# Gate logits as 2x2 block products of seven, their results summed in DRAM, in a one-core Trainium2 layer kernel

## The chip, the cores and the metric

The kernel runs on one core of a Trainium2 chip. It is one layer of a network in one launch, all in fp32, with every input and output in DRAM. The metric is the device time of the core in microseconds (us), lower is better. The engines are called as in the profile: PE is TensorE, DVE is VectorE, ACT is ScalarE, POOL is GpSimd, SP is SyncE, which issues most of the DMA transfers.

## The reference

The layer has 1024 tokens of 1024 channels. What matters here is its first sub-layer, two token mixers on one normalised input, each of them weighted by a gate per token and channel:

```python
h = rms_norm(x, norm_mix_pre)
proj = h @ w_in                 # q, k, v, u: 512 columns each; gate_logits: 2048
gate_attn, gate_ssm = jnp.split(jax.nn.sigmoid(gate_logits + b_gate), 2, axis=-1)
o_attn = stick_breaking_attention(q, k, v)      # 8 heads of 64
o_ssm = s5_branch(u, ...)       # 32 groups of 16 channels, 64 complex states; GELU, GLU
merged = gate_attn * (o_attn @ w_branch_attn) + gate_ssm * (o_ssm @ w_branch_ssm)
x = x + rms_norm(merged @ w_out, norm_mix_post)
```

Cross-attention into 256 memory tokens and a gated FFN with a causal convolution follow; the change leaves them as they are.

## The kernel before, in words

**Arithmetic.** A fp32 product is made of three matmuls on rounded operands: an operand is split into a high part, which ACT rounds, and a low part, which DVE makes as the difference; then come high x high, high x low and low x high (mm3, lines 141 to 143). One step of a projection is these three matmuls for 128 rows of the contraction, 128 output columns and 512 tokens. hT holds the normalised input, transposed, high and low. The norm's gain is in it, and the rate of a token (the reciprocal of its root mean square) is multiplied in later.

**A job** (class Job) is 128 columns of w_in: its weights are loaded (a tile ws), rounded (L255, ACT) and their low part is made (L259, DVE); 2 halves of 512 tokens by 8 steps of the contraction follow. There are 16 gate chunks, gate_job(0) to gate_job(15), 16 steps each. At the end of a half ACT copies the PSUM bank into a tile glog (L288), and SP stores it to g_d in DRAM. The merge, much later, loads g_d, multiplies the rates in and takes the sigmoid.

**The order of the work is written out by time.** at(t, go) puts a piece of work on a list with a planned time, and each engine's instructions are issued in the order of these times. The plan's times only set the order; on the chip an engine waits in that order for whatever its next instruction needs. Gate jobs are the filling between small matmuls that depend on other engines. Seven gate chunks fill the SSM (EARLY_SSM, 112 steps) and nine the attention (EARLY_ATT, 144 steps), in which the q and k projections fill too (128 steps).

**The stages**, by the profile's time: the v projection to 52 us; the projection of u, the SSM's input, to 92, beside which DVE prepares tables, operators and readouts of the SSM; the SSM to 218; the GLU to 241; the attention to 538; memory keys and values to 585; the merge to 673; then output projection, cross-attention and FFN.

**The SSM** goes in eight slots, one for four groups of channels (planned SLOT apart). In a slot: flip_u and flip_w (transposes); states (L732), eight matmuls; scan on DVE (L741 to L753), which reads their PSUM; outputs (L766, L767), planned 9.5 us after states, which read the scan's result rc. ACT puts the outputs through Gelu (L772). Every second slot, flip_y transposes eight blocks back (L783) and ACT copies them to U (L785). Between the slots' own work, for two slots at a time, DVE makes readout(n) (F, L678 to L680, three operations), operators(o) (W, L668 to L670, six operations) and tables(o) (cos and sin, L652 to L658, DVE and ACT). After the last flip_y, ACT and DVE split y into yh (L913) and yl (L916) for the GLU, whose matmuls are again lines 141 to 143.

**The attention** goes head by head. For each block of 256 queries: scores (L1004, L1005, PE), two sigmoids (L1016, L1017, ACT), a scan (L1022, DVE), a product (L1028, "rest", POOL), transposes (L1042, PE), the split of the weights into wth (L1049, ACT) and wtl (L1054, DVE), weigh (L1067, PE). Between these, in a fixed proportion, stand the fill steps.

Of the kernel before, what the change touches and what calls it, by code (L numbers as in the profile page):

```python
# [11 lines left out]
F32 = mybir.dt.float32  # L12
# [18 lines left out]
EARLY_SSM = (8, 9, 10, 11, 12, 13, 14)  # L31
EARLY_ATT = ((15, 0), (1, 2), (3, 4), (5, 6, 7))
# [13 lines left out]
def kernel(ctx: ExitStack, tc: tile.TileContext, a: dict, out: bass.AP, dbg=None):  # L46
# [35 lines left out]
    row_k = pr_.tile([P, 512], F32, name="row_k")  # L82
    rx_d = dpool.tile([KT, P], F32, name="rx_d")
# [199 lines left out]
    def gate_job(gi):  # L283
        def out(t, h, sl, acc):
            def put(t):
                pool, tag, bufs = logs[-1]
                gt = pool.tile([P, 512], F32, tag=tag, name="glog", bufs=bufs)
                C.copy(gt, acc)  # L288
                dma(g_d[gi][:, sl], gt)

            at(t, put)

        return Job(a["w_in_T"][8 + gi], out)

    def qk_job(pp, key):
# [28 lines left out]
        def start():  # L324

            qk[pp] = [[pqk.tile([P, S], F32R, tag=f"{n}{i}", name=f"{n}{i}") for i in range(2)] for n in ("q", "k", "kl")]
# [18 lines left out]
    px = wx.enter_context(tc.tile_pool(name="px", bufs=1, side="left"))  # L345
    rf, ra = ExitStack(), ExitStack()
    rf.enter_context(banks(f=(512, 2)))
    ra.enter_context(banks(keep="f", m=(512, 6)))
# [6 lines left out]
    logs.append((pa, "vt", 1))  # L355
# [7 lines left out]
    def x_load(t, kk=None):  # L363

        if t not in xt:
            xt[t] = p0.tile([P, KT, P], F32, tag="xt", name="xt", bufs=4)
# [7 lines left out]
    def w_load(n, c):  # L374
        raw[n, c] = px.tile([P, 1024], F32, tag="wr", name="wr", bufs=4)
        dma(raw[n, c], a["w_in_N"][n, c])
# [114 lines left out]
    def mem_load(i):  # L491
        raw["m", i] = px.tile([P, 1024], F32, tag="wr", name="wr", bufs=4)
# [11 lines left out]
    line(70.0, (lambda: mem_load(0), 0), (lambda: mem_load(1), 16.0), (lambda: mem_rate(0), 1.4), (lambda: mem_rate(1), 2.6),  # L504
# [132 lines left out]
    def open_t():  # L637
        r0.close()
        open_t.pool = rt.enter_context(tc.tile_pool(name="pt", bufs=1, side="right", reuse_waits="tile"))

    def tables(now, o):

        pool = open_t.pool
        x = pool.tile([P, 8, P], F32, tag="x", name="x")
        home, n_ = (open_b.pool, 1) if o == 2 else (pool, 2)
        cosT = home.tile([P, 8, P], F32, tag="cosT", name="cosT", bufs=n_)
        sinT = home.tile([P, 8, P], F32, tag="sinT", name="sinT", bufs=n_)
        tabs[o] = cosT, sinT
        G.memset(x[:, :, 0:1], 0.0)
# [1694 lines left out]
```

## Time and profile before

| | us |
|---|---|
| median of 3 runs (lowest, highest) | 1656.69 (1655.31, 1657.93) |
| span of the profiled execution | 1653.9 |
| PE busy | 1633.8 (99%) |
| DVE busy | 1163.6 (70%) |
| ACT busy | 880.1 (53%) |
| POOL busy | 202.2 (12%) |

The profile is of one further execution; its own time is its span, 1653.9 us from the first to the last instruction. A matmul's printed length includes its way through the array, so PE rows overlap: the distance between starts is what one costs. A window row gives, for a stretch of time, the busy time and the number of instructions of each engine, then PE's granted clock as a share of full speed (PEclk), the busy share of the DMA engines and what they moved. A row of the groups of instructions gives line, engine, operation, written and read tiles, shape and count, then busy us and the mean ns of one, then the idle time of the engine ahead of them and what ended it. In the chain, each row is one link: its start, its length and the work.

### The profile page before, as it was taken

To read this page: it belongs to the slowest core of one execution; us is meant where nothing else is said; L and a number is where in the kernel's file an instruction comes from. 1 tells how busy PE (TensorE), PEld (TensorE's weight loads), DVE (VectorE), ACT (ScalarE), POOL (GpSimd) and SP (SyncE) were. 2 spreads that over 40 slices of the span, in tenths; PEclk is the share of its full clock that TensorE was granted. 3 is DMA by queue.
4 is the path that set the end of the run, shared out by engine and by line. 5 is a ranking of instruction groups with operands and counts; after the bars stand their busy time and mean duration, and the time that the engine had idled before them with its cause. 6 is when DMAs were issued, how large, how long until landed. Compare 5 with 4: busy or idle time off the path is not lost.

```text
span 1653.9 us, 22415 instructions
## 1 busy us (share of the span) xinstructions
PE 1633.8 (99%) x8062; PEld 1379.8 (83%) x8062; DVE 1163.6 (70%) x1616; ACT 880.1 (53%) x1459; POOL 202.2 (12%) x296
## 2 busy tenths in 40 slices
PE   9999999999999999999999999999999999999998
PEld 7998887888888988888888888888888888888886
DVE  6778637776866687467655678888887788775473
ACT  5434346676766544344444556656565556654441
POOL 5000002333332000011000000111111111000010
PEclk9999999999999999999999999999999999999999
DMA  9412144232433954464423574677777676688672
GB/s 323 124 46 66 61 144 110 71 102 80 113 99 127 336 190 136 158 211 158 141 69 129 205 271 175 187 210 211 214 195 206 186 203 185 210 311 280 192 237 81
DMA packets 125439, 279.26 MB, mean 169 GB/s; under 512 B 23696, under 2 KB 28304, under 8 KB 125200
## 3 DMA queue, kind: packets, MB, share of 16 engines
q1 hardware_dynamic: 113664, 251.35, 46.1%
q0 software_dynamic: 9360, 18.09, 6.3%
q10 hardware_dynamic: 2304, 8.39, 1.3%
q8 instruction: 63, 1.03, 0.3%
q14 instruction: 48, 0.39, 0.1%
HBM read 203.98 MB, written 67.38 MB: 164 GB/s over the span
## 4 chain that ended last, share of the span: by engine, by line
PE 89%; DVE 6%; DMA 2%; ACT 2%; issue 1%; POOL 0%; SPq 0%; DVEq 0%; POOLq 0%; ACTq 0%
PE ps_p L1921 8%; PE ps_p L1919 8%; PE ps_p L1920 8%; PE ps_f L141 7%; PE ps_f L143 7%; PE ps_f L142 6%; PE ps_d L2190 4%; PE ps_d L2189 4%; PE ps_d L2191 4%; PE ps_m L141 3%; PE ps_m L143 3%; PE ps_m L142 3%; PE ps_o L1067 2%; PE ps_w L1042 2%; PE ps_z L141 1%; PE ps_z L142 1%
## 5 line engine op out<-in xcount | busy, mean ns | idle before, releaser
L141 PE MATMUL ps_f<-hT,wh 128*128 128x512 f32 x384 | 161.3, 420 | 0.0
L143 PE MATMUL ps_f<-hT,wl 128*128 128x512 f32 x384 | 150.8, 393 | 0.0
L142 PE MATMUL ps_f<-hT,wh 128*128 128x512 f32 x384 | 150.6, 392 | 0.0
L1920 PE MATMUL ps_p<-qS,bm 128*128 128x512 f32 (+2 forms) x368 | 140.4, 382 | 1.7 <-DVE qS L1744 1.7
L1919 PE MATMUL ps_p<-qS,bm 128*128 128x512 f32 (+2 forms) x368 | 140.5, 382 | 1.4 <-DVE uu L1937 0.9
L1921 PE MATMUL ps_p<-qS,bm 128*128 128x512 f32 (+2 forms) x368 | 140.5, 382 | 0.0
L147 DVE TENSOR_TENSOR dn<-raw,dn 128x1024 fp32r<-128x1024 f32 x77 | 93.4, 1223 | 63.0 <-ACT dn L146 59.2
L146 ACT CAST dn<-raw 128x1024 fp32r<-128x1024 f32 x77 | 80.5, 1054 | 87.2 <-PE ps_d L2191 36.4
L2189 PE MATMUL ps_d<-dn 128*128 128x512 f32 x308 | 119.8, 389 | 0.0
L2190 PE MATMUL ps_d<-dn 128*128 128x512 f32 x308 | 119.8, 389 | 0.0
L2191 PE MATMUL ps_d<-dn 128*128 128x512 f32 x308 | 119.8, 389 | 0.0
L1028 POOL TENSOR_TENSOR s<-s,s 128x127 f32<-128x127 f32 (+4 forms) x96 | 89.9, 937 | 223.8 <-DVE s L1022 178.6
L1921 PE MATMUL ps_p<-qA,bm 128*128 128x512 f32 (+2 forms) x272 | 105.1, 386 | 0.5 <-DVE bm L1850 0.5
L1919 PE MATMUL ps_p<-qA,bm 128*128 128x512 f32 (+2 forms) x272 | 105.3, 387 | 0.0
L1920 PE MATMUL ps_p<-qA,bm 128*128 128x512 f32 (+2 forms) x272 | 105.0, 386 | 0.0
L1932 ACT COPY uu<-ps_p 128x512 f32<-128x512 f32 (+2 forms) x90 | 51.5, 572 | 90.0 <-PE ps_p L1921 90.0
L1862 POOL DMA_DIRECT2D bm<-in_ffn_up_T x61 | 52.7, 864 | 356.6 <-ACT bm L1861 144.2
L143 PEld LDWEIGHTS ps_f<-hT,wl 128*128 128x128 f32 x384 | 72.1, 188 | 16.3
L1016 ACT ACTIVATE s<-ps_z,rates_x 128x128 f32<-128x128 f32 (+3 forms) x96 | 56.3, 587 | 54.0 <-PE ps_z L1005 47.8
L1919 PEld LDWEIGHTS ps_p<-qS,bm 128*128 128x128 f32 x368 | 69.2, 188 | 15.2 <-ACT uu L1932 2.2
L1920 PEld LDWEIGHTS ps_p<-qS,bm 128*128 128x128 f32 x368 | 69.2, 188 | 15.1 <-DVE qS L1744 2.0
L1921 PEld LDWEIGHTS ps_p<-qS,bm 128*128 128x128 f32 x368 | 69.3, 188 | 13.2
(544 smaller groups left out, 4462.2 us busy)
## 6 DMA issues: line engine op xcount, KB each, us to landing
raw<-sd SPq DMA_DIRECT2D x77, 256.0 KB, 3.5
bm<-in_ffn_up_T POOLq DMA_DIRECT2D x61, 256.0 KB, 5.4
ws<-in_w_in_T SPq DMA_DIRECT2D x24, 512.0 KB, 3.3
ws<-in_xa_wo_N SPq DMA_DIRECT2D x23, 512.0 KB, 4.3
wv<-in_ffn_up_T SPq DMA_DIRECT2D x22, 512.0 KB, 4.0
wg<-in_ffn_up_T SPq DMA_DIRECT2D x22, 512.0 KB, 3.8
dr<-in_ffn_down SPq DMA_DIRECT2D x22, 512.0 KB, 6.4
td<-st SPq DMA_DIRECT2D x44, 256.0 KB, 5.9
```

Source lines behind the costliest of these rows:

```text
L141: T.matmul(acc, sh, mh, start=first, stop=False)
L142: T.matmul(acc, sh, ml, start=False, stop=False)
L143: T.matmul(acc, sl, mh, start=False, stop=last)
L146: C.copy(dh, src)
L147: (lo or V).tensor_tensor(dl, src, f(dh), op=ALU.subtract)
L1028: G.tensor_tensor(s1[:, n0:e], s1[:, n0:e], s2[:, n0 + 1:e + 1], op=ALU.mult)
L1919: T.matmul(acc, bm[:, 0, ks], q[:, 0, k, cs], start=alone and k == 0, stop=False, skip_group_check=True)
L1920: T.matmul(acc, bm[:, 0, ks], q[:, 1, k, cs], start=False, stop=False, skip_group_check=True)
L1921: T.matmul(acc, bm[:, 1, ks], q[:, 0, k, cs], start=False, stop=k == 3, skip_group_check=True)
L2189: T.matmul(acc[i], v[:, 0, 0, sl], v[:, 0, 1], start=first, stop=False, skip_group_check=True)
L2190: T.matmul(acc[i], v[:, 0, 0, sl], v[:, 1, 1], start=False, stop=False, skip_group_check=True)
L2191: T.matmul(acc[i], v[:, 1, 0, sl], v[:, 0, 1], start=False, stop=last, skip_group_check=True)
```

## The change: gate chunks by pairs, seven products for eight

Two gate chunks (a pair: m = 0, 1), two halves of the tokens (th = 0, 1) and two halves of the contraction (4 steps each) are a 2x2 product of blocks. The new class Product does one of Strassen's seven products of such a pair: four steps of three matmuls (L428) on a sum of weight blocks and a sum of input blocks. 8 pairs x 7 products x 4 steps are 224 steps where there were 256.

- **Weight sums**: the second block is added by an accumulating load that POOL issues; for product 1 DVE makes the difference. Then ACT rounds (L401, L403) and DVE makes the low part (L407, L409), on 128x512.
- **Input sums** ("quads", for products 1, 2, 5, 6 and 7; 3 and 4 use hT): one at a time, from a new input x_Q, in one slot of a new pool that the x tiles of the first stage share. For 7 and 6 the second block is added by an accumulating load, and ACT and DVE scale and split. For 2, 5 and 1 ACT scales (4 operations), DVE adds (4), ACT rounds (4), DVE makes the low part (4).
- **Results**: a product goes to one or two of the four blocks of g_d. ACT copies it with its sign (L439, L441); the first contribution to a block is a plain store of SP, later ones are accumulating stores that POOL issues (52 of 54 of them in the attention). A copy whose two places have the same sign serves both. Odd chunks are kept negated, and the sigmoid's scale mends that. In the SSM products 4 and 7, or 3 and 6, of a pair share one PSUM accumulator and are copied once.
- **Places**: the SSM has 28 products (4, 7, 3, 6), 112 steps as before; the attention has 28 (first 2, with the q and k jobs between, then 5, then four of 3, then 1), 112 steps in place of 144.
- **To make room**: SLOT is 13.6 in place of 12.2, and outputs are planned 10.5 us after states in place of 9.5. readout 2 and 3 and operators 2 move from the u stage into SSM slots, tables 2 and 3 into slots 1 and 3. W has 2 buffers (3), F1 2 (4); r shares bp, x shares sinT, tq shares bt. PSUM m has 5 banks (6), a new g has 1. glog has 3 buffers in the SSM (1) and 2 in the attention as before. Some attention and memory tiles share buffers, and the merge's stage tiles are opened 25 us earlier.

```diff
-    def gate_job(gi):
...
+            for hh, d in enumerate(parts):
...
+    class Product:
...
+        def total(self, t):
+            if self.n == 1:
+                V.tensor_tensor(self.ws, self.ws, self.whole[:, 512:], op=ALU.subtract)
+            elif len(FACTOR[self.n]) == 2:
+                G.dma_start(self.ws, self.source(1), accum_op=ALU.add)
...
+            for j, (st, mv_) in enumerate(((wh, mh), (wh, ml), (wl, mh))):
+                T.matmul(self.acc, st, mv_, start=self.chain != "ends" and k == 0 and j == 0, stop=k == 3 and j == 2,
+                         skip_group_check=True)
...
+                gt = pool.tile([P, 512], F32, tag=tag, name="glog", bufs=bufs)
+                if sign < 0:
+                    C.mul(gt, self.acc, -1.0)
+                else:
+                    C.copy(gt, self.acc)
+                for th, m, adds in places:
+                    dst = g_d[2 * self.i + m][:, th * 512:(th + 1) * 512]
+                    if adds:
+                        at(t + 1.5, lambda _, dst=dst: G.dma_start(dst, gt, accum_op=ALU.add))
+                    else:
+                        dma(dst, gt)
...
-    SLOT = 12.2
+    SLOT = 13.6
...
-            plan(s0 + 9.5, 1.75, outputs, n)
+            plan(s0 + 10.5, 1.75, outputs, n)
...
-            if n == 0:
-                at(s0 + 8.5, lambda t: operators(t, 3))
-            if n == 1:
-                at(s0 + 8.5, lambda t: tables(t, 3))
+            if n in (0, 2):
+                at(s0 + 8.5, lambda t, n=n: operators(t, 2 + n // 2))
+            if n in (1, 3):
+                at(s0 + 8.5, lambda t, n=n: tables(t, 2 + n // 2))
...
+    quad(2, "w", clock + 9.0, (0.0, 13.0), 8.0)
...
+    fill_products(phase[3])
+    fill_products(phase[1])
```

On PE, at the end of the SSM, the order before was this (y is the last Gelu's output, hT and wh, wl a gate job's operands):

```order
L767 MATMUL ps_m<-F_1577,rc 128x128
L141 MATMUL ps_f<-hT_119,wh 128x512
L142 MATMUL ps_f<-hT_121,wh 128x512
L143 MATMUL ps_f<-hT_119,wl 128x512
L141 MATMUL ps_f<-hT_119,wh 128x512
L142 MATMUL ps_f<-hT_121,wh 128x512
L143 MATMUL ps_f<-hT_119,wl 128x512
L783 MATMUL ps_m<-ident,y_1819 128x128 x8
L141 MATMUL ps_f<-hT_119,wh 128x512
```

and 41 more matmuls of that gate job before the GLU's first. After the change, with S a quad and yh, yl the GLU's operands:

```order
L428 MATMUL ps_g<-S,bm 128x512 x12
L928 MATMUL ps_m<-Tt,Ug 128x128
L929 MATMUL ps_m<-F_1989,rc 128x128
L928 MATMUL ps_m<-Tt,Ug 128x128
L929 MATMUL ps_m<-F_1989,rc 128x128
L928 MATMUL ps_m<-Tt,Ug 128x128
L929 MATMUL ps_m<-F_1989,rc 128x128
L928 MATMUL ps_m<-Tt,Ug 128x128
L929 MATMUL ps_m<-F_1989,rc 128x128
L945 MATMUL ps_m<-ident,y_2027 128x128 x8
L141 MATMUL ps_f<-yh_2145,wh 128x512
L142 MATMUL ps_f<-yl_2146,wh 128x512
```

All filling now stands ahead of the last outputs, and the GLU stands right behind the last transposes.

On DVE, between two scans of the SSM (the one that ends in slot 2 and the next, whose first operation reads ps_m and cosT), before:

```order
L753 TENSOR_TENSOR rc<-rc,bt 128x4x127
L678 TENSOR_TENSOR F_1360<-pr,Y_164 128x512
L679 TENSOR_TENSOR tq<-pi,Y_165 128x512
L680 TENSOR_TENSOR F_1360<-F_1360,tq 128x512
L259 TENSOR_TENSOR wl<-ws,wh 128x1024
L741 TENSOR_TENSOR bp<-ps_m,cosT 128x512
```

and after, with bm the low part of a product's weights:

```order
L409 TENSOR_TENSOR bm<-ws,bm 128x512
L838 TENSOR_TENSOR F_1415<-pr,Y_171 128x512
L839 TENSOR_TENSOR tq<-pi,Y_172 128x512
L840 TENSOR_TENSOR F_1415<-F_1415,tq 128x512
L828 TENSOR_TENSOR W<-pr,X 128x512
L829 TENSOR_TENSOR tq<-pi,Xs 128x512
L830 TENSOR_TENSOR W<-W,tq 128x512
L828 TENSOR_TENSOR W<-pr,X 128x512
L829 TENSOR_TENSOR tq<-pi,Xs 128x512
L830 TENSOR_TENSOR W<-W,tq 128x512
L407 SCALAR_TENSOR_TENSOR bm<-ws,bm 128x512 x2
L903 TENSOR_TENSOR bp<-ps_m,cosT 128x512
```

The low part of 1024 columns became three of 512, and a set of operators (W) came in between.

On ACT in the attention, where the products 3 are (with what each instruction waits for: DMASW are DMA transfers that POOL issued, DMAHW those of SP), before:

```order
L1049 CAST wth<-ps_w 128x512 [waits DVE_49,PE_49,Activation_49]
L288 COPY glog<-ps_f 128x512 [waits DMAHW6_49,PE_49]
L1077 COPY oT<-ps_o 128x256 [waits PE_49]
L1016 ACTIVATE s_4508<-ps_z,rates_x 128x128 [waits PE_49,Pool_49]
L1017 ACTIVATE s_4507<-ps_z,rates_x 128x127
```

and after:

```order
L1249 COPY oT<-ps_o 128x256 [waits DMAHW0_49,DMAHW1_49,PE_49,Activation_49]
L439 ACTIVATE glog<-ps_f 128x512 [waits DMASW2_49,PE_49]
L441 COPY glog<-ps_f 128x512 [waits DMASW3_49]
L1221 CAST wth<-ps_w 128x256 [waits PE_49]
L1221 CAST wth<-ps_w 128x128
L403 CAST bm<-ws 128x512 [waits DMASW1_49]
```

Where one copy waited for a store of SP, two copies now wait for stores of POOL, and a split of attention weights (L1221) stands right behind them.

More of the change, by code (lines that the diff above doesn't have):

```diff
@@ L82 @@
     row_k = pr_.tile([P, 512], F32, name="row_k")
+    rsl = ExitStack()
+    psl = rsl.enter_context(tc.tile_pool(name="psl", bufs=1, side="left", reuse_waits="tile"))
     rx_d = dpool.tile([KT, P], F32, name="rx_d")
@@ L824 @@
     at(u_begin + 28.8, lambda t: operators(t, 1))
-    at(u_begin + 33.2, lambda t: readout(t, 2))
-    at(u_begin + 35.4, lambda t: readout(t, 3))
-    at(u_begin + 37.6, lambda t: operators(t, 2))
+    quad(7, "ws", u_begin + 6.0, (0.0, 5.0), 11.0)
     Tt = None
@@ L1134 @@
                 job.weights(t0)
+        elif isinstance(job, Product):
+            add = {1: 6.5, 3: 13.0}.get(job.n, 6.0)
+            job.weights(t0, add + 5.5, add, *((2.6, 1.3) if job is phase[3][1] else (5.0, 3.8)))
+            t1 = ended[phase[2 if job.n == 5 else 5][-1]]
+            if job is phase[5][0]:
+                quad(5, "w", t1 + 11.0, (0.0, 17.5))
+            elif job is phase[1][0]:
+                quad(1, "w", t1 + 0.8, (0.0, 3.0), 11.5)
         else:
@@ L1255 @@
     mem_at = clock
+    for n in range(4, 12):
+        at(mem_at - 24.0 + 4.0 * (n - 4), lambda _, n=n: G.memset(stage["012"[n // 4 - 1]][:, n % 4, 0:1], 0.0))
     def mem_k(now, ch, m, k):
```

263 lines of the change are left out of this document (203 added, 60 removed).

## The prediction

> **What bounds the kernel now.** I read the page first, then the chain of waits, then the windows by stage, and last the timelines of the places that the change touches.
>
> ```profile
> span 1653.9 us, 22415 instructions
> PE 1633.8 (99%) x8062; PEld 1379.8 (83%) x8062; DVE 1163.6 (70%) x1616; ACT 880.1 (53%) x1459; POOL 202.2 (12%) x296
> PE 89%; DVE 6%; DMA 2%; ACT 2%; issue 1%; POOL 0%; SPq 0%; DVEq 0%; POOLq 0%; ACTq 0%
> ```
>
> TensorE is busy in 99% of the span and carries 89% of the chain that ended last. The whole kernel has 20 us in which TensorE does nothing. So a matmul taken out is time taken out, unless its place is filled by a wait. The question is how well the other engines keep up once it is gone, so I look at the stages one by one (columns: window, its length, then busy us and count of PE, weight loads, DVE, ACT, POOL; granted clock, DMA share, GB/s).
>
> ```profile
> core 0: us, PE busy (x) PEld busy (x) DVE busy (x) ACT busy (x) POOL busy (x), PEclk, DMA share, GB/s
> 52.00:92.00 40.00, 40.00 (x174) 39.58 (x173) 33.09 (x59) 16.48 (x21) 2.71 (x7) 1.00 0.32 53
> 92.00:218.00 126.00, 125.33 (x717) 110.52 (x717) 91.07 (x151) 52.66 (x69) 1.19 (x9) 1.00 0.20 64
> 218.00:241.00 23.00, 23.00 (x100) 18.55 (x99) 7.97 (x11) 9.18 (x13) 0.00 (x0) 1.00 0.44 158
> 241.00:538.00 297.00, 295.29 (x1633) 251.19 (x1633) 209.66 (x279) 200.96 (x417) 92.19 (x159) 1.00 0.36 103
> ```
>
> These are the projection of the SSM's input, the SSM with gate steps as filling, the GLU, and the attention with the other gate steps as filling. TensorE idles 0.7 us in the SSM and 1.7 us in the attention. VectorE has 28% and 29% left there.
>
> **The change part by part.** The sum is made against the profiled execution, whose span of 1653.9 us is 2.8 us below the median of the runs, 1656.7; I add those 2.8 at the end.
>
> *Steps that go.* A fill step is three 128x512 matmuls. Between two first matmuls of a step six steps apart (start, length, engine, line):
>
> ```profile
> 206.40 0.39 PE L767 MATMUL ps_m<-F,rc 128*128 128x128 f32 x2
> 208.02 1.03 PE L783 MATMUL ps_m<-ident,y 128*128 128x128 f32 x8
> 213.00 0.39 PE L141 MATMUL ps_f<-hT,wh 128*128 128x512 f32 x1
> 217.08 0.39 PE L141 MATMUL ps_f<-hT,wh 128*128 128x512 f32 x1
> 212.52 1.22 DVE L916 TENSOR_TENSOR yl<-U,yh 128x1024 fp32r<-128x1024 f32 x1 [1.77 <-ACT yh L913]
> ```
>
> From 213.00 to 217.08 is 4.08 us, 0.68 a step. Sixteen chunks of 16 steps are 256 steps before; 8 pairs of 7 products of 4 steps are 224 after. The SSM keeps its 112 steps (28 products for 7 chunks), the attention goes from 144 to 112. 32 x 0.68 = **-21.8 us**, all from the attention.
>
> *VectorE in the SSM's slots.* Each of the eight slots begins with matmuls for the states, on which a scan on VectorE waits, on which the outputs' matmuls wait. This is the chain there, through scans 1 and 2 (start us, length us, engine, tile, line):
>
> ```profile
> 122.28 0.91 PE ps_m L732 x8
> 123.20 0.69 DVE bp L741
> 130.18 0.28 DVE ktt L691
> 132.20 0.61 DVE tq L679
> 133.64 0.19 DVE x L652
> 136.58 1.23 DVE x L654
> 137.81 0.60 DVE bp L741
> 144.09 0.70 DVE rc L753
> 144.93 0.46 PE ps_m L767 x2
> ```
>
> A scan is 137.81 to 144.79, 7.0 us. The states' matmuls are 0.92 us ahead of it. Outputs are planned 9.5 us after the states' start, 10.5 after the change, so a scan may be late by 10.5 - 7.9 = 2.6 us. In this trace, one was late: VectorE had the intra term, a chunk's low part, a readout and a set of tables (133.64 to 137.81, 4.2 us) to do first, and TensorE waited for the end of scan 2 until 144.93. The change lengthens a slot of TensorE from 12.2 to 13.6 us, but fills VectorE more: the low part of a product is one operation on 128x512, as are the six of a set of operators and the three of a readout.
>
> ```profile
> L670 DVE TENSOR_TENSOR W<-W,tq 128x512 f32<-128x512 f32 x4 | 2.8, 694 | 0.1
> ```
>
> With 0.69 us each, slot 0 holds a scan, 4 lows and operators: 7.0 + 2.75 + 4.15 = 13.9. Slot 1: scan, 0.28, 3 lows, readout, tables: 7.0 + 0.3 + 2.1 + 2.1 + 4.2 = 15.7. Slot 2: scan, 3 lows, readout, operators: 15.35. Slot 3 is as slot 1, 15.7. Slot 4: scan, 3 lows, readout and the four lows of quad 6: 13.95. Over 13.6 these are 0.3 + 2.1 + 1.75 + 2.1 + 0.35 = 6.6 us; slots 5 to 7 have room. Less the 2.6 of slack, TensorE waits **+4.0 us** (0 if the late scans of slots 0 to 4 find room in what the plan has spare, 6.6 if no slack is there). The 0.7 idle us of before are of the same kind and in this number, **-0.7**.
>
> *The end of the SSM.* Before, the last outputs (L767, 206.40) were followed by 6 and then 42 matmuls of filling until 218, during which ScalarE and VectorE did Gelu, the transposed copies, and the y parts. The last low part of y starts at 212.52 and ends at 213.74, 7.2 us behind the outputs' end at 206.54. With slots of 13.6 us the filling is used up: in the changed order nothing stands between the outputs and the GLU but the eight transposes. What TensorE can do in those 7.2 us is the transposes (208.02 to 208.81, 0.8) and the three GLU steps that don't need the last part of y (2.1): it idles 7.2 - 2.9 = **+4.3 us** (2 if more GLU steps are free of that part; 7.2 if none).
>
> *The clock behind that gap.* The trace has one place with a similar lull, before the FFN, and the granted clock behind it:
>
> ```profile
> 1022.00:1028.00 6.00, 4.91 (x42) 4.63 (x41) 5.33 (x10) 4.14 (x10) 0.00 (x0) 1.00 0.00 0
> 1028.00:1031.00 3.00, 2.37 (x21) 2.37 (x22) 2.96 (x5) 1.07 (x3) 0.00 (x0) 1.00 0.24 68
> 1031.00:1035.00 4.00, 4.00 (x14) 3.23 (x14) 3.97 (x8) 1.69 (x6) 0.00 (x0) 0.57 0.53 211
> ```
>
> After 9 us with 1.7 idle, four us were granted 0.57: 4 x 0.43 = **+1.7 us** if the end of the SSM does the same (0 to 1.7). The Trainium skill, TensorE: Matmul & The Clock Gate, in "Why this matters for your kernels", asks for no gap of TensorE above some 3 us between bursts. By that rule gaps cut up by transposes and GLU steps cost no clock, and the sum would be 1.7 us lower; the row above, with shorter gaps than that, speaks against it, so I keep the 1.7.
>
> *Copies of chained products.* Products 4 and 7, or 3 and 6, share an accumulator, and 30 copies on ScalarE leave the SSM's PSUM instead of 14. With 52.66 us of 126 busy, 16 x 0.59 = 9.4 us more finds room. With three banks for products of 2.7 us a late copy stops the third one: **+1.0** (0 to 3).
>
> *The attention.* TensorE's 297 us become 275. The other engines get more in less time (rows of this stage for the two copies, of the whole kernel for the others):
>
> ```profile
> L255 ACT CAST wh<-ws 128x1024 fp32r<-128x1024 f32 x16 | 16.9, 1056 | 0.0
> L288 ACT COPY glog<-ps_f 128x512 f32<-128x512 f32 x18 | 10.6, 589 | 6.4 <-PE ps_f L143 5.9
> L259 DVE TENSOR_TENSOR wl<-ws,wh 128x1024 fp32r<-128x1024 f32 (+1 forms) x28 | 34.1, 1217 | 18.7 <-ACT wh L255 18.6
> L146 ACT CAST bm<-t 128x512 fp32r<-128x512 f32 x85 | 52.7, 621 | 32.2 <-PE ps_p L1921 27.8 <-DVE t L1826 4.3
> L147 DVE TENSOR_TENSOR bm<-t,bm 128x512 fp32r<-128x512 f32 x85 | 58.2, 686 | 0.0
> L1862 POOL DMA_DIRECT2D bm<-in_ffn_up_T x61 | 52.7, 864 | 356.6 <-ACT bm L1861 144.2
> ```
>
> ScalarE: 201.0 - 9 x 1.06 (roundings of nine chunks) + 28 x 0.62 (of products) + 14 x 0.59 (32 copies for 18) + 16 x 0.62 (quads 5 and 1) = 227, 83% of 275. VectorE: 209.7 - 9 x 1.22 + 28 x 0.69 + 8 x 0.69 (differences of product 1) + 16 x 0.69 (quads) = 234, 85%. POOL: 92 + 56 DMA issues x 0.86 = 140, 51%. No engine becomes the bound by its sum. But the queues get fuller; if waits grow as u/(1-u), from 71% to 85%, the 1.7 idle us become 4.1, **+2.4**, an estimate (bounds -1.7, when the new order waits nowhere, and +10).
>
> Then there is a new wait. Copies go through two buffers, and a copy waits until the store out of its buffer has landed. Stores were plain ones of SP; now 52 of them are accumulating ones of POOL, and in phase 3 (the four products 3) each product has two copies, so that each one waits for the product before. Behind the waiting copy on ScalarE stand roundings of attention weights, and for these VectorE and then TensorE wait:
>
> ```profile
> g_d<-glog SPq DMA_DIRECT2D x32, 256.0 KB, 2.0
> DMA to landing us min/median/max: 3.8/5.4/8.2
> stb<-ol_d POOLq DMA_DIRECT2D x4, 512.0 KB, 8.7
> 432.52 0.59 ACT L1049 CAST wth<-ps_w 128x512 fp32r<-128x512 f32 x1 [0.75 <-PE ps_w L1042]
> 433.14 0.69 DVE L1054 TENSOR_TENSOR wtl<-ps_w,wth 128x512 fp32r<-128x512 f32 x1 [0.93 <-ACT wth L1049]
> 436.81 0.48 PE ps_o L1067 x4
> ```
>
> The second row answers for line 1862, the FFN's accumulating loads of the same 256 KB, with the DMA engines busier than the 0.36 of the attention; no accumulating store is in this trace. I take 4.5 us, between its least and its median. A round is then a copy (0.6), one POOL operation ahead (0.9) and 4.5, 6.0 us, against 4.6 for a product (275 us for 112 product and 128 q and k steps, four steps). TensorE needed the example's weights 436.81 - 433.83 = 3.0 us after they were done, so some 2.8 us of lateness are covered, once. Four products: 4 x 1.4 - 2.8 = **+2.8** (0 with 2.0 or 3.8; 6.4 with 5.4; the 8.7 row is a rival below). The Trainium skill, DMA: Bandwidth & Descriptors, "Anatomy of one DMA — SWDGE (gpsimd) path", fits 2.0 us plus bytes over 436e3 for such a DMA; that is an estimate of 2.6 us here, a round of 4.1, no wait, and a sum lower by 2.8. The landings above are twice that, so I don't take it.
>
> *At nothing.* Quad 7 and the first lows lie in the 52 to 92 window, from which two readouts and a set of operators leave (8.3 us of VectorE) for some 5 us that come. Quad 2 lies beside the GLU: 5.5 us more for VectorE's 7.97 of 23. Without that cover each would cost at most its own 5 us. The other buffers (shared slots, r in bp, sin in x) make orders that VectorE has anyway, since one engine does both sides. The accumulating loads of weight sums start 13 us ahead in the SSM, and 6 in the attention against 5.4.
>
> *Sum.* -21.8 + 4.0 - 0.7 + 4.3 + 1.7 + 1.0 + 2.4 + 2.8 = -6.3: a span of 1647.6, and with the 2.8, **1650.4 us**.
>
> **The rivals.** *Gain kept.* VectorE's lateness in the SSM is taken up and the attention's copies never wait: -21.8 - 0.7 + 4.3 + 1.7 + 1.0 = -15.5, 1641.2 us. For it: the attention's engines have 40 us each left, and landings at 3.8 need no wait. Against: scan 2 already waits in this trace with less in its slot. Chance 0.20.
>
> *Gain eaten.* Landings at the 5.4 median (+3.6 over the forecast) and no slack in the SSM (+2.6): 1650.4 + 6.2 = 1656.6, no change. For it: both are a row's own value. Against: the busier DMA engines of that row. Chance 0.24, for 1653.4 to 1660.
>
> *Slower, by late landings.* If accumulating into DRAM takes 8.7 us as the row of line stb does, a round is 10.2 us: phase 3 waits 4 x 5.6 - 2.8 = 19.6 us, and the other 24 products, with one copy each, 24 x (10.2 - 9.2) / 2 = 12. That is 31.6 in place of 2.8: 1679 us. It turns slower than now by over 0.2% from landings of some 7.3 us (4 x 4.2 - 2.8 = 14). For it: a store that adds must read DRAM, add and write; 8.2 occurred. Against: that row moved 512 KB. Chance 0.16.
>
> That the change doesn't do what it says is excluded by the changed order, which has 96 fill matmuls less.
>
> **How the numbers follow.** The forecast (1645 to 1653.4) has 0.40. A measurement of this kernel can tell about 0.2%, 3.3 us, from no change. Faster by more: forecast and gain kept, 0.60; within: 0.24; slower: 0.16. The range from 1640 to 1662 leaves out some 0.06 below (terms of the tail at nothing too) and some 0.13 of the late landings. The forecast's own range is 1645 to 1653.4.
>
> **What would show it.** Right: TensorE's busy time down by 22 us; idle of some 4 us between the last outputs (L929) and the first GLU steps with a granted clock below 1 behind; scans 2 to 5 that begin late, and outputs waiting for rc; copies L439 and L441 that wait for landings in phase 3 only. Wrong: idle in all heads of the attention released by ScalarE or VectorE, copies that wait in each product, landings of g_d above 7 us, or an attention stage still near 297 us; on the other side, no wait of outputs for rc, and a tail without idle.

## The result: slower by 2.7%

The changed kernel takes 1701.18 us (median of four runs, 1700.17 to 1701.71), 1656.15 for the kernel before: a ratio of 1.0268 (95% interval 1.0254 to 1.0283). The forecast was 1650.4, the range 1640 to 1662. The page of the profile after, the lines that answer to those of before:

```profile
span 1699.5 us, 22783 instructions
PE 1638.9 (96%) x7966; PEld 1371.9 (81%) x7966; DVE 1222.0 (72%) x1696; ACT 929.9 (55%) x1563; POOL 280.6 (17%) x394
PE 76%; DVE 11%; DMA 6%; ACT 5%; issue 2%; POOL 0%; SPq 0%; DVEq 0%; ACTq 0%; POOLq 0%
```

TensorE has the 96 matmuls less (8062 to 7966), and idles 60.6 us where it idled 20.1. Its busy time rose all the same, in good part since matmuls at a lower clock count longer. DMA transfers, VectorE and ScalarE now hold 22% of the chain.

To see where the time went, I cut both traces at the same four places of the program: the first states, the last outputs, the first scores and the last weigh. Before (the columns are those of the windows in the prediction):

```profile
60.00:110.10 50.10, 50.10 (x222) 48.83 (x222) 32.63 (x62) 18.48 (x24) 2.71 (x7) 1.00 0.21 58
110.10:204.80 94.70, 94.03 (x565) 82.39 (x564) 77.77 (x133) 38.94 (x51) 0.74 (x7) 1.00 0.19 63
204.80:255.80 51.00, 51.00 (x235) 42.04 (x234) 19.14 (x24) 21.64 (x30) 0.45 (x2) 1.00 0.44 140
255.80:537.30 281.50, 279.79 (x1563) 238.25 (x1561) 204.28 (x272) 196.37 (x408) 92.19 (x159) 1.00 0.34 99
```

and after:

```profile
60.00:117.40 57.40, 52.65 (x220) 50.27 (x220) 25.27 (x47) 22.10 (x31) 9.08 (x12) 0.94 0.53 123
117.40:236.30 118.90, 110.37 (x613) 91.91 (x612) 99.85 (x175) 61.17 (x93) 21.71 (x33) 0.99 0.76 186
236.30:282.00 45.70, 43.00 (x188) 34.02 (x187) 23.64 (x31) 25.32 (x36) 0.45 (x2) 0.96 0.58 188
282.00:580.40 298.40, 271.51 (x1466) 224.86 (x1465) 242.50 (x315) 216.23 (x457) 140.40 (x221) 0.98 0.69 162
```

In all four stretches TensorE now idles (length less busy time: 4.8, 8.5, 2.7 and 26.9 us, where it was 0, 0.7, 0 and 1.7), and the granted clock is below 1. The DMA share rose from 0.19 to 0.76 in the SSM and doubled in the attention. The next table sets each stretch against what TensorE's work alone would give:

| stretch | before | TensorE's work after | after | lost |
|---|---|---|---|---|
| to the first states | 110.1 | 110.1 | 117.4 | 7.3 |
| SSM, first states to last outputs | 94.7 | 105.6 (10.9 of filling came in from behind the outputs) | 118.9 | 13.3 |
| last outputs to first scores | 51.0 | 40.1 | 45.7 | 5.6 |
| attention, first scores to last weigh | 281.5 | 259.7 (less 21.8) | 298.4 | 38.7 |
| the rest | 1116.6 | 1116.6 | 1119.0 | 2.4 |

That is 67.3 us lost and 21.8 gained, and makes the 45.6 us between the two spans.

### The profile page after: what moved, and what is told of

It reads as the page before. It is cut to its first block, busy times and chain, and to the rows that moved or that the text cites. A ratio compares the mean times of both kernels' runs of the same rounds, so it can differ in the third digit from the quotient of the medians.

```text
span 1699.5 us, 22783 instructions
## 1 busy us (share of the span) xinstructions
PE 1638.9 (96%) x7966; PEld 1371.9 (81%) x7966; DVE 1222.0 (72%) x1696; ACT 929.9 (55%) x1563; POOL 280.6 (17%) x394
## 4 chain that ended last, share of the span: by engine, by line
PE 76%; DVE 11%; DMA 6%; ACT 5%; issue 2%; POOL 0%; SPq 0%; DVEq 0%; ACTq 0%; POOLq 0%
PE ps_p L2125 8%; PE ps_p L2126 8%; PE ps_p L2124 8%; PE ps_d L2396 4%; PE ps_d L2394 4%; PE ps_d L2395 4%; PE ps_f L428 4%; PE ps_f L141 3%; PE ps_f L142 3%; PE ps_f L143 3%; PE ps_m L141 2%; PE ps_m L142 2%; PE ps_m L143 2%; PE ps_o L1239 2%; PE ps_z L142 1%
## 5 line engine op out<-in xcount | busy, mean ns | idle before, releaser
L1200 POOL TENSOR_TENSOR s<-s,s 128x127 f32<-128x127 f32 (+4 forms) x96 | 99.8, 1047 | 169.3 <-DVE s L1194 135.2
L428 PE MATMUL ps_f<-S,bm 128*128 128x512 f32 x420 | 120.1, 407 | 2.6 <-DVE bm L407 0.9
L2124 PE MATMUL ps_p<-qA,bm 128*128 128x512 f32 (+2 forms) x272 | 105.6, 388 | 0.0
L428 PEld LDWEIGHTS ps_f<-S,bm 128*128 128x128 f32 x420 | 73.8, 190 | 16.0 <-DVE bm L409 1.3
L2126 PEld LDWEIGHTS ps_p<-qS,bm 128*128 128x128 f32 x368 | 70.3, 191 | 13.3 <-DVE bm L2055 0.2
L1194 DVE TENSOR_TENSOR_SCAN s<-s,begin 128x128 f32<-128x128 f32 (+1 forms) x64 | 62.5, 978 | 15.1 <-ACT s L1188 14.5
L146 ACT CAST bm<-t 128x512 fp32r<-128x512 f32 x85 | 52.8, 622 | 32.7 <-PE ps_p L2126 28.6
```

The costliest lines, as they stand in the source:

```text
L146: C.copy(dh, src)
L428: T.matmul(self.acc, st, mv_, start=self.chain != "ends" and k == 0 and j == 0, stop=k == 3 and j == 2, skip_group_check=True)
L1200: G.tensor_tensor(s1[:, n0:e], s1[:, n0:e], s2[:, n0 + 1:e + 1], op=ALU.mult)
L2124: T.matmul(acc, bm[:, 0, ks], q[:, 0, k, cs], start=alone and k == 0, stop=False, skip_group_check=True)
L2126: T.matmul(acc, bm[:, 1, ks], q[:, 0, k, cs], start=False, stop=k == 3, skip_group_check=True)
```

## The waits in the trace after

**Ahead of the first states.** The chain of waits there (start, length, what):

```profile
50.39 12.30 DMA rx_d<-rates_x
62.75 7.29 DMA r<-rx_d
...
70.80 0.81 ACT S L341
71.63 1.46 DVE S L349 x2
...
81.87 0.70 DVE W L830
82.62 1.89 PE ps_m L846 x8
```

The tokens' rates go through DRAM. They came back at 70 us (the load of r took 1.8 us before), with the two accumulating loads of x_Q for quad 7, 512 KB each, on the way at the same time; these landed some 18 us after their issue at 50.3. ScalarE's copies of U wait for them, the high parts of quad 7 stand behind these copies, the low parts stand at the head of VectorE's queue, and tables and operators behind them. TensorE needs W at 76.6 and gets it at 80.8.

**In the SSM.** What TensorE waited for here (the list of waits, PE's own rows: us, times, longest):

```profile
PE ps_m L893 <- ACT Ug L880: 2.6, 2, 2.0
PE ps_g L428 <- DVE bm L407: 2.1, 2, 1.7
PE ps_f L428 <- DVE bm L409: 2.0, 2, 1.6
...
PE ps_g L428 <- DVE bm L409: 1.0, 1, 1.0
PE ps_f L428 <- DVE bm L407: 0.9, 1, 0.9
```

Some 6 us are low parts of products, made late by VectorE, and 2.6 are inputs of the states, copied late by ScalarE. No output (L928, L929) waited for a scan. One low part behind a scan (L914 is near the scan's end, L407 the low part, L428 the product), and one PE row of slot 5's first states:

```profile
216.76 0.69 DVE bt L914
...
218.08 0.69 DVE bm L407
218.82 2.60 PE ps_f L428 x10
```

```profile
194.55 0.71 PE L893 MATMUL ps_m<-Ug,E 128*128 128x128 f32 x4 [2.01 <-ACT Ug L880]
```

The product could have begun at 217.96 but for its low part, which stood behind seven microseconds of scan. The states at 194.55, after a slot of 17.8 us (slot 4), waited for a copy on ScalarE, whose queue ahead of it read (timeline of ScalarE):

```profile
182.82 1.06 ACT L816 ACTIVATE cosT<-sinT 128x1024 f32<-128x1024 f32 x1
183.79 1.51 ACT L341 ACTIVATE S<-xq,zcol,gcol 128x512 fp32r<-128x512 f32 x2
185.31 1.28 ACT L817 ACT_TABLE_LOAD   x1
186.61 1.06 ACT L817 ACTIVATE sinT<-sinT 128x1024 f32<-128x1024 f32 x1
...
188.08 1.15 ACT L818 ACTIVATE cosT<-cosT,hpi 128x1024 f32<-128x1024 f32 x1
...
190.07 1.52 ACT L341 ACTIVATE S<-xq,zcol,gcol 128x512 fp32r<-128x512 f32 x2
191.61 1.28 ACT L934 ACT_TABLE_LOAD   x1
192.91 0.60 ACT L934 ACTIVATE y<-ps_m 128x512 f32<-128x512 f32 x1
```

These are the last set of tables, with its change of function table and the change back, and quad 6 between.

**In the attention.** The list of waits (engine, line, what it waited for: us, times, longest) and the DMA rows (KB each, us to landing):

```profile
PEld ps_o L1239 <- DVE wtl L1226: 17.1, 16, 2.5
ACT oT L1249 <- DMA ol_d<-oT: 16.2, 6, 4.7
PE ps_o L1239 <- DVE wtl L1226: 13.4, 14, 2.3
...
ACT glog L441 <- DMA g_d<-glog: 7.0, 3, 3.2
...
ACT glog L439 <- DMA g_d<-glog: 1.8, 3, 1.4
```

```profile
g_d<-glog POOLq DMA_DIRECT2D x54, 256.0 KB, 6.1
...
ws<-in_w_in_T POOLq DMA_DIRECT2D x32, 256.0 KB, 5.7
...
xq<-in_x_Q POOLq DMA_DIRECT2D x4, 512.0 KB, 13.7
```

TensorE waits for the attention's own weights (wtl), made by VectorE late. ScalarE in its turn waits for stores: of copies of products, and longer of the attention's output, whose tile oT had two buffers before and has one now. The change takes that buffer away, though the description of it ahead of the prediction doesn't list it.

## The experiments

Theory 1 was late landings of DMA transfers, above all the accumulating ones; theory 2 full engines, VectorE above all; theory 3 the single buffer of the attention's output. The last four columns of the table are the same four stretches, in us, each from one profiled execution. The SSM's carries up to 3.4 us of chance: the lull in slot 4 is followed by 3.4, 6.8 or 10.2 us of half clock, in kernels with the same code there. What lies behind the last weigh took 1115 to 1125 us in all kernels but q_latesum, nearly without edits there, so a few us in the whole say little; an edit is read from its own stretch first.

| kernel | us | ratio to before (95%) | first states | SSM | outputs to scores | attention |
|---|---|---|---|---|---|---|
| before | 1656.2 | | 110.1 | 94.7 | 51.0 | 281.5 |
| after | 1701.2 | 1.0254 to 1.0283 | 117.4 | 118.9 | 45.7 | 298.4 |
| a_stores | 1691.8 | 1.0179 to 1.0241 | 117.5 | 122.2 | 45.7 | 281.6 |
| b_wsums | 1699.6 | 1.0227 to 1.0287 | 118.8 | 120.5 | 44.2 | 298.4 |
| c_stages | 1708.8 | 1.0276 to 1.0349 | 118.4 | 120.6 | 44.2 | 304.1 |
| d_oT | 1695.2 | 1.0201 to 1.0260 | 116.8 | 118.9 | 44.2 | 289.0 |
| e_quad7 | 1692.8 | 1.0176 to 1.0259 | 109.8 | 122.1 | 44.2 | 297.8 |
| f_slot | 1698.3 | 1.0221 to 1.0280 | 117.3 | 112.1 | 49.9 | 298.3 |
| g_lows | 1695.0 | 1.0201 to 1.0260 | 118.3 | 116.5 | 44.2 | 294.4 |
| h_lows_att | 1698.0 | 1.0219 to 1.0279 | 118.2 | 122.1 | 45.8 | 286.9 |
| i_three | 1676.0 | 1.0089 to 1.0147 | 116.9 | 120.5 | 44.2 | 270.4 |
| k_mends | 1689.8 | 1.0153 to 1.0250 | 110.2 | 112.1 | 49.8 | 293.8 |
| l_quad6 | 1692.8 | 1.0190 to 1.0249 | 117.0 | 113.6 | 44.3 | 295.4 |
| m_pool | 1685.0 | 1.0138 to 1.0207 | 117.8 | 122.2 | 45.7 | 282.2 |
| n_tables3 | 1687.2 | 1.0164 to 1.0224 | 118.2 | 107.6 | 44.2 | 297.7 |
| o_quads | 1671.4 | 1.0069 to 1.0127 | 118.5 | 122.1 | 45.7 | 263.6 |
| p_lead | 1695.4 | 1.0214 to 1.0273 | 117.6 | 116.9 | 44.2 | 299.3 |
| q_mends | 1684.3 | 1.0146 to 1.0187 | 110.0 | 115.4 | 44.2 | 293.6 |
| q_latesum | 1718.9 | 1.0361 to 1.0395 | 109.5 | 113.8 | 44.2 | 276.0 |

**The stores, plain.**

```diff
-                        at(t + 1.5, lambda _, dst=dst: G.dma_start(dst, gt, accum_op=ALU.add))
+                        dma(s_d[len(later_)], gt)
+                        later_.append(0)
```

> All 54 later contributions to the gate logits go as plain stores of SP, each into a place of its own, and are not added (the gate logits are incomplete). Theory 1, late landings: copies on ScalarE wait for accumulating stores, and their traffic makes other transfers land late; the attention (first scores to last weigh) falls from 298 us to 275 or less and the whole to about 1677 us. Theory 2, full engines: ScalarE and VectorE simply have too much in too little time; the attention stays above 290 and the whole above 1693.

The attention fell by 16.8 us, to 281.6, between the two expectations (275 or less, or above 290), and the whole by 9. So the stores are a cause and not all of it: 22 of the 39 us were left.

**The stores, plain, but through POOL.**

```diff
-                        at(t + 1.5, lambda _, dst=dst: G.dma_start(dst, gt, accum_op=ALU.add))
+                        at(t + 1.5, lambda _, n=len(later_): G.dma_start(s_d[n], gt))
+                        later_.append(0)
```

> The later contributions still go through POOL's queue, at the same places, but as plain stores, each into a place of its own (not added). If it is POOL's issuing (0.9 us each, ahead of its products for the attention's weights) that costs, the attention stays at 295 to 300 us. If it is the adding, by late landings and its traffic, it falls to 282 as with SP's plain stores.

282.2 us: the same as with SP. POOL's 54 issues cost nothing that can be seen; the adding does. The DMA row of this kernel:

```profile
s_d<-glog POOLq DMA_DIRECT2D x54, 256.0 KB, 3.7
```

The same 256 KB from the same queue land in 3.7 us unadded and in 6.1 added. Other stores gain too, here those of the attention's output, first in the change, then in this kernel, and ScalarE's wait for them falls from 16.2 us to 8.0:

```profile
ol_d<-oT SPq DMA_DIRECT2D x16, 128.0 KB, 4.2
```

```profile
ol_d<-oT SPq DMA_DIRECT2D x16, 128.0 KB, 2.7
ACT oT L1251 <- DMA ol_d<-oT: 8.0, 5, 2.5
```

**No weight sums.**

```diff
-            elif len(FACTOR[self.n]) == 2:
-                G.dma_start(self.ws, self.source(1), accum_op=ALU.add)
```

> The accumulating loads that make the weight sums are left out (products of two weight blocks use the first alone). Theory 1, late landings: the products in the SSM wait for weights that come in two transfers one after the other; the SSM (first states to last outputs) falls from 119 us to about 109 and the whole to about 1690 us. Theory 2, VectorE is behind in the SSM's slots: the SSM stays at 116 or more, the whole above 1697.

Nothing moved (120.5 and 298.4 us). The weights, in two transfers one behind the other, landed in time. Theory 1 falls for the SSM.

**Stage tiles opened late.**

```diff
-    at(clock - 25.0, lambda _: stages())
+    at(clock + 0.1, lambda _: stages())
-    for n in range(4, 12):
-        at(mem_at - 24.0 + 4.0 * (n - 4), lambda _, n=n: G.memset(stage["012"[n // 4 - 1]][:, n % 4, 0:1], 0.0))
```

> The merge's stage tiles are opened when they were before, not 25 us earlier, and POOL's memsets that pace the loads of memory weights are left out. If these early loads crowd the DMA engines at the end of the attention, its last head falls from 32 us to about 26 and the whole by 4 to 8 us. If not, the whole stays within 3 us of 1701, or rises because the memory stage waits for its weights.

A miss: the attention got 5.7 us longer and the whole 7.6. The edit took away POOL's memsets, which hold the loads of the memory weights back, together with the early opening, and the trace shows what followed: eight of these loads, 512 KB each, were issued between 470 and 501 us, where the change issues the first at 549.1. From 470 to 510 us the DMA engines moved 296 GB/s in place of 227, and from 510 to 550 TensorE was busy for 30.9 us in place of 34.9. So this run speaks for crowded DMA engines as a cost in the attention; what the early opening costs by itself it doesn't show.

**The output's buffer in two halves.**

```diff
-            if c % 2 == 0:
-                half[n] = pat.tile([P, 512], F32, tag="oT", name="oT", bufs=1)
...
+            oT = pat.tile([P, 256], F32, tag="oT", name="oT", bufs=2)
+            C.copy(oT, o_ps[:, :256])
...
```

> The one buffer for the attention's output, of 512 queries, becomes two of 256, each stored by itself: the same memory, but a copy no longer waits for the store just before it. Theory 3, the single buffer: ScalarE's 16 us of waiting for these stores go and the whole falls by 6 to 12 us. If these waits were covered: within 3 us of 1701.

The attention fell by 9.4 us, the whole by 6, and the wait of L1249 for stores was gone from the list: theory 3 holds for so much.

**No low parts in the attention.**

```diff
         def low(self, t):
+            if self.home_att:
+                return
...
-            wh, wl = (self.bm[:, j, k * P:(k + 1) * P] for j in range(2))
+            wh, wl = (self.bm[:, 0 if self.home_att else j, k * P:(k + 1) * P] for j in range(2))
```

> VectorE makes no low parts and no differences for the products of the attention; the matmuls take the high part (36 operations of 0.69 us less, the same matmuls). Theory 2, full engines: the attention falls from 298 us to 280 or less, the whole to about 1683. Theory 1, late landings (the plain stores took 17 us of the attention's 39): the attention stays at 290 or more, the whole above 1692.

286.9, between the two again: 11.5 us are VectorE's load, 25 us of work taken off it (28 low parts and 8 differences). The whole fell by 3 only, since in this run the SSM and the rest came out 3 us longer each.

**These three at once** (a_stores, d_oT and h_lows_att together).

> Three edits on the attention at once: later contributions stored plainly by SP (not added), the output's buffer in two halves, no low parts and differences on VectorE. Alone they took 17, 9 and 11.5 us off its 298. If the three are separate causes, the attention falls to about 261 us, TensorE's own time for it (281.5 less 21.8), and the whole to about 1664. If they are one wait seen three times, it stays at 275 or more and the whole above 1678.

270.4 us: 28.0 saved where the three alone make 16.8 + 9.4 + 11.5 = 37.7. They are not one wait, nor wholly separate: a store that lands early also frees oT (ScalarE's 16.2 us of waiting for it are 8.0 in m_pool), and VectorE waits less for ScalarE when ScalarE waits less (L1226 for L1221: 22.4 us in the change, 14.7 in d_oT).

**And no quads 5 and 1 in the attention**, on top of i_three.

```diff
-                quad(5, "w", t1 + 11.0, (0.0, 17.5))
+                at(t1 + 11.0, lambda _: quads.__setitem__(5, quads[2]))
...
-                quad(1, "w", t1 + 0.8, (0.0, 3.0), 11.5)
+                at(t1 + 0.8, lambda _: quads.__setitem__(1, quads[2]))
```

> On top of i_three (plain stores, two halves of the output's buffer, no low parts in the attention) quads 5 and 1 are left out (the products use quad 2; same matmuls). i_three left the attention at 270 us, 11 over TensorE's own 260. If the quads' 16 + 16 operations and their 4 MB of loads are the rest: 260 to 263 and the whole about 1667. If the rest lies elsewhere (the start of the attention, the copies): 267 or more.

263.6 us, 4 over TensorE's own 259.7. The windows of these two kernels' attention:

```profile
281.70:552.10 270.40, 260.65 (x1466) 220.40 (x1465) 211.48 (x279) 217.83 (x457) 95.05 (x171) 1.00 0.60 175
```

```profile
286.40:550.00 263.60, 259.05 (x1467) 220.44 (x1465) 199.33 (x263) 207.74 (x441) 92.87 (x171) 1.00 0.55 163
```

VectorE at 199 of 264 us and ScalarE at 208 leave TensorE busy 98% of the stage; at 242 and 216 of 298, as in the change, it idles 27 us. So the gain of 21.8 us is there once the change's own work in this stage is left out: stores that add, the single oT, low parts and quads take it.

**Quad 7 later.**

```diff
-    quad(7, "ws", u_begin + 6.0, (0.0, 5.0), 11.0)
+    quad(7, "ws", u_begin + 16.0, (0.0, 5.0), 11.0)
```

> Quad 7 is planned 10 us later, behind the first tables and operators on VectorE; nothing is left out. If its low parts held up VectorE while the token rates were still on their way through DRAM, the first states come at 110 us in place of 117.4, TensorE's 4.8 us of waiting for W and the half clock behind it go, and the whole falls by 5 to 8 us. If the rates' own late landing is the cause, the first states stay at 117.

The first states came at 109.8, the whole fell by 8. The window ahead of them:

```profile
60.00:109.80 49.80, 49.80 (x221) 48.54 (x221) 25.22 (x47) 21.89 (x31) 10.06 (x14) 1.00 0.63 141
```

No idle and no half clock are left, although the rates took 12.0 and 7.0 us, nearly as in the change (12.3 and 7.3). The order of the queues was the cause, not the landing itself.

**A shorter slot.**

```diff
-    SLOT = 13.6
+    SLOT = 12.2
```

> SLOT is 12.2 again, so that about 16 steps of products are left for the time behind the last outputs; nothing is left out. If the chain of engines in the slots sets the SSM's pace, first states to last outputs stays at 117 to 119 us, the 11 us of products go behind the outputs and cover the gap there: last outputs to first scores gets no more than 6 us longer, and the whole changes by +-4 us. If TensorE's filling sets the pace, the SSM falls by 10 us and the whole by 4 to 6.

Between the two: the SSM 6.8 us shorter, the stretch behind it 4.2 longer, the whole 2.9 less, at the edge of what two runs tell. So the slots were not set by TensorE's filling alone: it idles 12.5 us in the shorter SSM (8.5 in the change). The 42 matmuls that went behind the last outputs covered the gap there, where TensorE no longer idles (2.7 us in the change).

**No low parts in the SSM** (the edit of h_lows_att, for the SSM's products).

> VectorE makes no low parts for the products of the SSM; the matmuls take the high part in their place (28 operations of 0.69 us less, the same matmuls). Theory 2, VectorE in the slots: the SSM falls from 119 us to 106 to 109 and the whole to about 1690 us. If it is ScalarE (copies, tables, quad 6), the SSM stays at 114 or more and the whole above 1695.

A miss as to size: 116.5 us, with 10.2 us of half clock in it where the change had 3.4. The slots tell more: the first four took 55.4 us in place of 59.3 (planned 54.4), the fifth 17.8 as in the change. TensorE idled 4.3 us in place of 8.5.

**Nor quad 6**, on top of g_lows.

```diff
-                    quad(6, "w", clock + 0.6, (0.0, 4.0), 11.5)
+                    at(clock + 0.6, lambda _: quads.__setitem__(6, quads[7]))
```

> No low parts on VectorE in the SSM as in g_lows, and quad 6 is left out as well (the products 6 use quad 7; same matmuls). If the long slot of 18 us is ScalarE's with quad 6 and tables 3 in one slot, it falls to 14 us, the SSM from 116.5 to about 106 to 108 with no half clock in it, and the whole to about 1685. If not, the slot stays at 17 or more.

The slot still took 16.6 us, between the two expectations. Quad 6, which I had blamed, gives 1.2.

**Nor the last tables**, on top of l_quad6.

```diff
-            if n in (1, 3):
-                at(s0 + 8.5, lambda t, n=n: tables(t, 2 + n // 2))
+            if n == 1:
+                at(s0 + 8.5, lambda t: tables(t, 2))
+            if n == 3:
+                at(s0 + 8.5, lambda t: tabs.__setitem__(3, tabs[2]))
```

> On top of l_quad6 (no low parts, no quad 6 in the SSM) the last set of tables is left out (the last two slots use the set before). Leaving quad 6 out took only 1 us off the slot of 18. If ScalarE's row of tables 3 (three activations and two table loads, 5.7 us) is what holds Gelu and the next slot's input there, slot 4 falls from 16.6 to 14 us and the SSM from 113.6 to 106 to 108, the half clock gone. If not, the slot stays at 16 or more and another wait holds it.

The slot took 13.8 us and the SSM 107.6, without half clock:

```profile
118.20:225.80 107.60, 106.96 (x614) 91.16 (x613) 78.52 (x138) 52.84 (x84) 19.87 (x30) 1.00 0.75 188
```

The tables were left out on both engines, so this doesn't part ScalarE's 5.8 us from VectorE's 4.2; that ScalarE's copy was what the states waited for, the row at 194.55 above shows. With low parts, quad and tables gone, TensorE is busy in all but 0.6 us, at a DMA share of 0.75: the transfers don't hold up the SSM. It is still 2.0 us above the 105.6 of TensorE's work; 1.4 of these are not explained.

**Weights earlier in the order.**

```diff
-                    first_of[ns].weights(clock)
+                    first_of[ns].weights(clock, 20.5, 16.0, 9.2, 8.0)
```

> Nothing left out: in the SSM the weights of all products but the first are loaded, rounded and split 3 us earlier in the order, so that fewer low parts stand behind a scan on VectorE. If their place in the order costs, the SSM falls from 119 to 122 us to 116 or less and the whole to about 1696. If it is VectorE's sum of work, another piece is late in their stead: within 2 us of 1701.

SSM 116.9, just above the 116 asked for, with 10.2 us of half clock in it where the change had 3.4; the whole 5.7 us less than the change, of which the SSM shows 2.0. The first four slots and the rest of the SSM:

```profile
117.60:174.00 56.40, 55.04 (x323) 46.85 (x321) 52.73 (x97) 29.27 (x45) 12.83 (x20) 1.00 0.81 208
174.00:234.50 60.50, 57.31 (x291) 48.49 (x292) 46.29 (x78) 30.63 (x46) 9.01 (x13) 0.92 0.72 174
```

TensorE idled 4.5 us in them, where it idled 8.5 in the change and 4.3 without any low parts. The first four slots took 56.4 us (55.4 without low parts), at the same work of VectorE: the place of the low parts behind the scans was the cost, more than VectorE's sum.

**The mends together**: k_mends (e_quad7, f_slot, d_oT) and q_mends (e_quad7, p_lead, d_oT).

> The three mends that keep the result together: quad 7 planned 10 us later, SLOT 12.2, the output's buffer in two halves. Alone they gave 7, 3 and 6 us. If they add up: about 1685 us, still slower than before by 28. If the waits that they take away come back elsewhere: 1690 or more.

> Three mends with nothing left out: quad 7 planned 10 us later, the SSM's weights 3 us earlier in the order, the output's buffer in two halves. Alone they gave 8, 6 and 6 us. If they add up: about 1681 us. If waits come back elsewhere: 1688 or more.

11 and 17 us of the 17 and 20 that their parts gave alone; k_mends at the edge of its second expectation, q_mends between its two. Both are slower than before still.

**Adding in the merge**: q_mends, with plain stores and this in the merge, the gates loaded 7 us earlier:

```diff
+    def gate_add(d, h, n):
+        for br in range(2):
+            for x in later_.get(((8 if br == 0 else 0) + d, h), [])[n:n + 1]:
+                G.dma_start(gates[d, h][br], s_d[x], accum_op=ALU.add)
```

> The same three mends, and the later contributions go as plain stores of SP to places of their own and are added by accumulating loads of POOL in the merge, where POOL is idle; nothing is left out. The attention should fall to about 272 us, as with plain stores and the halved buffer alone, the whole to about 1665 us, if the 54 loads are hidden beside the merge's 88 us of matmuls. If the merge waits for them (up to three one after the other of some 5.5 us for one gate), it gets 10 to 30 us longer and the whole stays at 1675 or more.

The attention took 276.0 us, 22 less than the change, with the adding moved out of it; but the rest took 1171.1 in place of 1119.0, where 10 to 30 more had been expected at worst. In the merge the scaling of the gates waits for the added loads:

```profile
ACT gt L1520 <- DVE gt L1516: 80.9, 22, 14.7
DVE gt L1516 <- DMA gt<-s_d: 51.7, 11, 12.5
```

What was saved in one stage was paid more than twice in the other. No kernel here beats the one before.

## Why the prediction was wrong

It took the bound and the gain rightly and the costs too low, point by point:

- **Steps that go, -21.8**: right. 96 matmuls are gone, and the attention runs at 263.6 us against 281.5 when its new work is taken away.
- **The end of the SSM, +4.3, and its clock, +1.7**: right in the total, 5.6 us lost against 6.0, and in ScalarE's and VectorE's waits that were named; the row's clock of 0.96 in 45.7 us is 1.8. The idle time was 2.7 us and not 4.3, so part of the agreement is luck.
- **Quad 7 "at nothing"**: wrong, 7.3 us. I compared sums in the window, where VectorE has room, and not what stands ahead of what: the low parts waited for DRAM, by way of ScalarE's queue, with the operators behind them.
- **VectorE in the slots, +4.0**: VectorE was late, as forecast, but the wait was wrong and so was the total, 13.3 with the clock. The sum has outputs wait for a late scan; no output did. TensorE waited some 6 us for products' low parts, which stand behind an undivided scan, and the place of these, more than VectorE's sum, was what counted (p_lead). Nor do the slots follow the sum: slots 1 and 3 were to be 2.1 us late and slot 4 0.35; over 13.6 they were late by 0.15, 1.2 and 4.2. In slot 4 the states waited for ScalarE, for which the sum had only its copies: the moved tables with two function-table loads made that slot last 17.8 us.
- **Copies of chained products, +1.0**: nothing of it shows. No wait of TensorE for such a copy is in the SSM's list.
- **Accumulating stores, +2.8**: mis-sized, 17. They landed in 6.1 us, not 4.5, and my own formula gives 9 for that (4 x 3.0 - 2.8). ScalarE did wait for them, 8.8 us, about where it was forecast: at the last products 3 and the first products 1 (nearly all from 522 to 546 us). What the formula left out is that the adding made other stores late: the attention's output store landed in 4.2 us, in 2.7 with plain stores (m_pool), and ScalarE waited 16.2 us for it, 8.0 in m_pool. How much of the 17 each of the two makes was not parted. By the fit of the Trainium skill, DMA: Bandwidth & Descriptors ("Anatomy of one DMA — SWDGE (gpsimd) path"), an estimate of 2.6 us, there would have been no wait; the trace is at more than twice that.
- **Queues, +2.4**: mis-sized. The sums of work were near (ScalarE 216 us for 227, VectorE 242 for 234, POOL 140 for 140), and still low parts cost 11.5 us by themselves, and quads 5 and 1 some 7 more when the other three were gone.
- **The second buffer of oT**, taken away by the change, is not named in the sum: 9.4 us alone. It could be read ahead of the run: in the orders of ScalarE above, L1077 waits for PE alone, and L1249 for two stores of SP as well.
- **The clock**: one episode priced, six came in the four stretches. PEclk in their windows makes 0.06 x 57.4 + 0.01 x 118.9 + 0.04 x 45.7 + 0.02 x 298.4 = 12 us, at 1.00 before; it is part of the 67.3 us. This was nowhere in the sums of the other waits. The last idle stretches ahead of the episodes were 0.8 to 4.2 us; the Trainium skill, TensorE: Matmul & The Clock Gate ("Why this matters for your kernels"), puts the limit at some 3 us between bursts. The trace shows less to be enough in places (2.0 at 192.5). In others it was not: 2.3 us at 480.2 and 1.9 at 521.4 were followed by no half clock. What decides between them stays open.

The third rival named the right direction and one of the mechanisms, late landings. But by its own sum the kernel turns slower only from landings of some 7.3 us, and they took 6.1: the direction came from the other costs together with this one. Of the signs of being wrong, the attention still near 297 us came (298.4); landings of g_d above 7 us and copies that wait in each product did not.

What stays open: the attention's last 4 us; what the early opening of the stage tiles costs; and how much of the tables' slot is each engine's.

## What to carry to other kernels

Where TensorE is 99% busy, as here, the other engines are hidden only by their place in their queues, and a saving of matmuls can be spent by the work that pays for it: cost each new operation by what stands in front of it and behind it in its queue, not by the free share of its engine. Price a lull of TensorE as time and, possibly, as half clock behind it. Buffers given up to make room are part of the price, above all those that a store must leave.

## What the runs showed of the hardware

An accumulating store of 256 KB landed in 6.1 us, a plain one from the same queue in 3.7, from SP's in 2.9 (a_stores). Half clock came in stretches of 3.4, 6.8 and 10.2 us behind idle stretches of 0.8 to 4.2 us, not behind every one of 2 us, and how long differed between kernels with the same code there. Issuing 54 transfers from POOL in place of SP cost nothing that shows in the attention (282.2 us in m_pool, 281.6 in a_stores).
